# Decay rows three chunks ahead in five buffers, and six PSUM banks for the q/k/v projection, in a hybrid DeltaNet / SGU / Fourier layer

## The chip, the cores and the metric

The kernel runs on one core of a Trainium2 chip. The metric is the device time of one execution in microseconds (us). Engines are named as in the profile: PE is TensorE (matrix multiply), PEld its weight loads, DVE is VectorE, ACT is ScalarE, POOL is GpSimd, and SP is SyncE, which here only issues DMAs. Each engine works through its own instruction queue in order: an instruction that waits holds back everything behind it on its engine.

## The reference, cut to what matters

One layer processes 2048 sample tokens and 128 prompt tokens (2176 in all, D_MODEL = 1024). A combined projection feeds three token mixers (gated DeltaNet, a spatial-gating MLP, a Fourier mixer), which are gated, merged and projected out. The change lies in the preparation of the DeltaNet branch:

```python
qkv = short_conv(qkv, conv_w).astype(jnp.float32)      # qkv: 1536 columns of the projection, conv over 3 tokens, SiLU
...
g = -jnp.exp(a_log) * jax.nn.softplus(dec + dt_bias)   # log decay per token, direction and head
...
gam = jnp.cumsum(gc, axis=-1)                          # running sum inside a chunk
diff = gam[..., :, None] - gam[..., None, :]
dec_incl = jnp.where(incl, jnp.exp(jnp.where(incl, diff, 0.0)), 0.0)
```

`dec_incl` is a triangular matrix of decays for each chunk, direction (forward and backward) and head. The kernel works in chunks of 128 tokens: 17 chunks, 2 directions, 4 heads, so 17 x 8 matrices of 128 x 128.

## The kernel before, in words

**Stages.** The tokens are normalised and kept as two 16-bit halves, `xh` and `xl`; each projection is three matmuls per 128 rows of contraction (line 160, `mm`, called from `gemm_T`). After a first stage (the `z_a` gate) comes the **q/k/v stage**, lines 488 to 510: twelve column tiles `ct` of 128 channels. For each, five token blocks `TBS` (four of 512 tokens and one of 128) are multiplied into a PSUM bank of the pool `ps_mm`, which has three; ACT copies the bank to `raw` (line 500, under a higher priority), which frees it. Then come three DVE operations of the convolution (lines 503 to 505), a sigmoid on ACT in four pieces (line 508), a product on POOL in four pieces (line 509) and a DMA to DRAM (line 510). `raw` and `cy` have two buffers each. Three further PSUM pools of one bank each, `ps_chain`, `ps_lev` and `ps_out`, are handed out in turn by `bank(ps_d, ...)`; two more banks are `ps_x`.

**Decays.** The generator `decays()` (lines 403 to 485) runs beside the q/k/v stage. It computes `gam` (kept in the tile `tok`), writes it to DRAM as rows (`gamR`, line 470), and then goes through the 17 chunks. For a chunk it broadcasts the rows of `gamR` to all 128 partitions with two DMAs of 256 KB from the SP queue (line 478), runs eight 128 x 128 `scalar_tensor_tensor` on DVE (line 481: subtract `gam` of the token on the partition, then take the minimum with the triangle `neg_f` or `neg_b`), the exponential on ACT (line 483, 128 x 1024) and a DMA of 512 KB to DRAM from the ACT queue (line 484). The row buffers are two: tile `dc` for odd chunks, half of tile `XB` for even ones. Both tiles serve later steps as well (`prep`, line 537, and `base_inverse`, line 595), as do the tiles `E` and `Et` of 128 x 1024, which belong to `base_inverse` alone.

**Weights.** Each column tile needs a weight tile: `load_w` (line 180) loads 512 KB by a DMA on the SP queue into `wst` (line 183), ACT sums its squares (line 187), DVE casts the sum (line 170, `wscb`), PE adds it over the partitions with a 128 x 1 matmul (in the trace `b<-wscb,ones`), DVE forms the scale (lines 173 to 177), ACT and DVE write the two 16-bit halves (lines 189 and 190). `getw(1, 2)` at the head of a column tile asks for weights two tiles ahead.

**What sets the order.** The text of the program gives each instruction a priority by its place. `pace.tick(tn / 100)` after a block adds to an account, and each 1.2 in it advances `decays()` to its next `yield`, so that the text mixes the two. The order of each engine's queue is then fixed when the kernel is built, by a planner that keeps a clock of its own for every engine, takes what it believes ready, and prefers the earlier in the text; on the chip the queues run in that order whatever the real times are. After the stage `pace.drain()` empties `decays()`, and `delta()` (preparation of each chunk, block inverses, and the two scans) is paced in the same way beside the SGU, the Fourier and the merge stages.

Of the kernel before, what the change touches and what calls it, by code (L numbers as in the profile page):

```python
# [15 lines left out]
ALU = mybir.AluOpType  # L16
# [4 lines left out]
P = 128  # L21
# [5 lines left out]
NCH = NTOK // P  # L27
H = 4
# [5 lines left out]
XB = 4  # L34
# [11 lines left out]
_COFF = {}  # L46
# [64 lines left out]
def hybrid_flow_kernel(ctx: ExitStack, tc: tile.TileContext, x_prompt, x_sample, state_delta, c, c_ctx, ln_g, w_ada,  # L111
# [3 lines left out]
    V, A, G, PE, SY = nc.vector, nc.scalar, nc.gpsimd, nc.tensor, nc.sync  # L115
# [9 lines left out]
    def sb(pl, shape, tag, dt=F32, bufs=None):  # L125
        kw = {} if bufs is None else {"bufs": bufs}
        return pl.tile(list(shape), dt, tag=tag, name=nm(tag), **kw)
# [5 lines left out]
    ps_mm = pool(ctx, "ps_mm", 3, space=PSUM)  # L133
    ps_d = [pool(ctx, f"ps_d{i}", 1, space=PSUM) for i in range(3)]
# [4 lines left out]
    def bank(pl, shape, tag="b"):  # L139
        if pl is ps_d:  # L140
            rot[0] += 1
            pl = ps_d[rot[0] % 3]
        return pl.tile(list(shape), F32, tag=tag, name=nm(tag))
# [6 lines left out]
    cst = sb(csp, [P, _CF], "cst")  # L150
    SY.dma_start(cst, consts[:, 0:_CF])
    K = {n_: cst[:, a:b] for n_, (a, b) in _COFF.items() if b <= _CF}
# [162 lines left out]
    for blk in range(8):  # L315
# [3 lines left out]
        ps = bank(ps_d, [2, 256])  # L319
# [38 lines left out]
    for ti, (t0, tn) in enumerate(TBS):  # L358
# [13 lines left out]
        for k in range(KT):  # L372
            ps = bank(ps_d, [P, tn])
            for j in range(nt):
                PE.transpose(ps[:, j * P:(j + 1) * P], xt[:, j, k * P:(k + 1) * P], ident)
            t = sb(p0p, [P, tn], "xm", bufs=3)
# [3 lines left out]
        for g in range(4):  # L380
            ps = bank(ps_mm, [P, tn])
# [18 lines left out]
    dq = pool(dl, "dqa", 1, side="right")  # L400
    a1 = ExitStack()
    a1p = pool(a1, "a1p", 2)
    def decays():
        pbs = sb(dq, [P, NCH, 16], "sq")
        for c0, c1 in ((0, 9), (9, NCH)):
            pb = bank(ps_mm, [P, c1 - c0, 32])
            for t in range(c0, c1):
                ts = slice(t * P, (t + 1) * P)
                for k in range(KT):
                    if k == KT - 1:  # L410
                        mm(pb[:, t - c0, 0:16], xl[:, k, ts], bdp[:, k, 0:16], False, False)
                    mm(pb[:, t - c0, :], xh[:, k, ts], bdp[:, k, :], k == 0, k == KT - 1)
                    if k < KT - 1:
                        mm(pb[:, t - c0, 0:16], xl[:, k, ts], bdp[:, k, 0:16], False, False)
            A.copy(pbs[:, c0:c1, :], pb[:, :, 16:32])
            V.tensor_tensor(pbs[:, c0:c1, :], pbs[:, c0:c1, :], pb[:, :, 0:16], ALU.add)
        pbv = pbs.rearrange("p c (s d h) -> p s d c h", s=2, d=2)
        for d in range(2):
            A.activation(beta[:, d], pbv[:, 0, d], AF.Sigmoid, scale=bdw.inv)
        yield 1  # L420
        NH = 2 * NCH * H
        blob = sb(dq, [P, 2, WB], "tok").rearrange("p d x -> p (d x)")
        dec, e0, e1, e2 = [blob[:, i * 160:i * 160 + NH] for i in range(4)]
        dec = dec.rearrange("p (d c h) -> p d c h", d=2, h=H)
        for d in range(2):
            V.tensor_scalar(dec[:, d], pbv[:, 1, d], bdw.inv, None, ALU.mult)
        dtb = sb(a1p, [P, 2, H], "dtb", bufs=1)
        al = sb(a1p, [P, 2, H], "al", bufs=1)
        SY.dma_start(dtb, dt_bias.rearrange("o d h -> o (d h)").to_broadcast([P, 8]).rearrange("p (d h) -> p d h", d=2))
        SY.dma_start(al, a_log.rearrange("o d h -> o (d h)").to_broadcast([P, 8]).rearrange("p (d h) -> p d h", d=2))  # L430
        A.activation(al, al, AF.Exp)
        for d in range(2):
            V.tensor_tensor(dec[:, d], dec[:, d], dtb[:, d, :].rearrange("p (o h) -> p o h", o=1).to_broadcast([P, NCH, H]), ALU.add)
        flat = lambda t: t.rearrange("p d c h -> p (d c h)")
        V.scalar_tensor_tensor(e0, flat(dec), -1.0, flat(dec), ALU.mult, ALU.max)
        A.activation(e0, e0, AF.Exp, scale=-1.0)
        V.tensor_scalar(e1, e0, 1.0, None, ALU.add)
        A.activation(e2, e1, AF.Ln)
        V.tensor_scalar(e1, e1, -1.0, 1e-30, ALU.add, ALU.max)
        V.reciprocal(e1, e1)  # L440
        V.tensor_mul(e2, e2, e1)
        V.tensor_scalar(e1, e0, -0.5, 1.0, ALU.mult, ALU.add)
        V.tensor_tensor(e2, e2, e1, ALU.max)
        V.tensor_mul(e2, e2, e0)
        V.scalar_tensor_tensor(e2, flat(dec), 0.0, e2, ALU.max, ALU.add)
        yield 1
        gg = e1.rearrange("p (d c h) -> p d c h", d=2, h=H)
        for d in range(2):
            V.scalar_tensor_tensor(gg[:, d], e2.rearrange("p (d c h) -> p d c h", d=2, h=H)[:, d], -1.0,
                                   al[:, d, :].rearrange("p (o h) -> p o h", o=1).to_broadcast([P, NCH, H]), ALU.mult, ALU.mult)  # L450
        pg = bank(ps_d, [P, 2, NH])
        HN = NH // 2
        for d, tri in ((0, "tri_f"), (1, "tri_b")):
            mm(pg[:, 0, d * HN:(d + 1) * HN], K[tri], flat(gg)[:, d * HN:(d + 1) * HN])
        mm(pg[:, 1, :], ones, flat(gg))
        gam = e0.rearrange("p (d c h) -> p d c h", d=2, h=H)
        V.tensor_copy(flat(gam), pg[:, 0, :])
        A.activation(flat(eg), flat(gam), AF.Exp)
        A.activation(flat(egl), pg[:, 1, :], AF.Exp)
        V.tensor_tensor(flat(ed), pg[:, 1, :], flat(gam), ALU.subtract)  # L460
        A.activation(flat(ed), flat(ed), AF.Exp)
        V.tensor_scalar(flat(neg), flat(eg), -1.0, None, ALU.mult)
        yield 1
        gamR = dram("gamR", [2, NCH * H, P])
        for d in range(2):
            pt = bank(ps_d, [HN, P])
            PE.transpose(pt, flat(gam)[:, d * HN:(d + 1) * HN], ident)
            gr = sb(a1p, [HN, P], "gr", bufs=1)
            V.tensor_copy(gr, pt)
            SY.dma_start(gamR[d], gr)  # L470
        for t in range(NCH):
            if t % 2:
                row = sb(dq, [P, 2, WB], "dc")
            else:
                row = sb(dq, [P, 2048], "XB")[:, 0:1024].rearrange("p (d x) -> p d x", d=2)
            row = row.rearrange("p d (h i) -> p d h i", h=H)
            for d in range(2):
                SY.dma_start(row[:, d], gamR[d, t * H:(t + 1) * H, :].rearrange("h (o i) -> o h i", o=1).to_broadcast([P, H, P]))
            for d in range(2):
                for h in range(H):  # L480
                    V.scalar_tensor_tensor(row[:, d, h, :], row[:, d, h, :], gam[:, d, t, h:h + 1], K["neg_f" if d == 0 else "neg_b"], ALU.subtract, ALU.min)
            yield 1
            A.activation(row, row, AF.Exp)
            A.dma_start(decD[t], row.rearrange("p d h i -> p d (h i)"))
            yield 1

    pace.start(decays(), 1.2)
    for ct in range(12):
        w = getw(1, 2)
        for half in range(1):  # L490
            raw = sb(a1p, [P, LP], "raw")
            G.memset(raw[:, 0:1], 0.0)
            G.memset(raw[:, NS + 1:NS + 3], 0.0)
            G.memset(raw[:, LP - 1:LP], 0.0)
            for t0, tn in TBS:
                ps = bank(ps_mm, [P, tn])
                gemm_T(ps, w, 0, xh[:, :, t0:t0 + tn], xl[:, :, t0:t0 + tn])
                o = t0 + 1 if t0 < NS else t0 + 3
                with tc.high_priority():
                    A.activation(raw[:, o:o + tn], ps, AF.Copy, scale=w.inv)  # L500
                pace.tick(tn / 100)
            y = sb(a1p, [P, LP - 2], "cy")
            V.tensor_scalar(y, raw[:, 0:LP - 2], convw(0, ct), None, ALU.mult)
            V.scalar_tensor_tensor(y, raw[:, 1:LP - 1], convw(1, ct), y, ALU.mult, ALU.add)
            V.scalar_tensor_tensor(y, raw[:, 2:LP], convw(2, ct), y, ALU.mult, ALU.add)
            for c0 in range(0, LP - 2, CQ):
                c1 = min(c0 + CQ, LP - 2)
                A.activation(raw[:, 1 + c0:1 + c1], y[:, c0:c1], AF.Sigmoid)  # L508
                G.tensor_tensor(y[:, c0:c1], y[:, c0:c1], raw[:, 1 + c0:1 + c1], ALU.mult)  # L509
            G.dma_start(qkvD[ct], y)  # L510
# [350 lines left out]
    ps = bank(ps_x, [P, 4, P])  # L861
# [6 lines left out]
    for t in range(NCH):  # L868
        ps = bank(ps_mm, [P, 4, P])
# [10 lines left out]
        ps = bank(ps_x, [P, 4, P])  # L880
# [7 lines left out]
    for g in range(4):  # L888
        uw, zw = getw(2, 2)
        for ti, (t0, tn) in enumerate(TBS):  # L890
            st = sb(ep, [P, tn], "st", bufs=3)
            SY.dma_start(st, vsD[g][:, t0:t0 + tn])
            ps = bank(ps_mm, [P, tn])
# [17 lines left out]
    for g in range(4):  # L911
        xw, zw = getw(2, 2)
        for gh in range(1):
            yT = sb(fp, [P, NTOK], "yT", bufs=1)
            Y1 = sb(fp, [P, 64, 32], "Y1")
            for q in range(0, NCH, 4):
                qn = min(4, NCH - q)
                ps = bank(ps_mm, [P, qn, P])
                for i in range(qn):
                    t = q + i  # L920
# [4 lines left out]
                if q < 16:  # L925
                    ps = bank(ps_x, [P, 4, 64, 2])
# [3 lines left out]
                else:  # L930
                    ps = bank(ps_x, [P, 2 * P])
# [225 lines left out]
```

## Time and profile before

| | before |
|---|---|
| runs | 2378.42 us median of 3 (2374.1 to 2380.57) |
| profiled execution | 2377.82 us, of which the span from first to last instruction is 2376.0 us |
| mean granted TensorE clock | 0.981 |
| HBM read and written | 222.16 MB and 125.39 MB |
| q/k/v stage, first to last matmul | 153.57 to 444.04 us |
| chunks of `decays()`, first DVE operation to last store issued | 188.0 to 309.9 us |

A profile page gives, for the slowest core, the busy time of each engine, groups of instructions by line with their count, total and mean time, and the idle time of the engine just before them with what ended it. "x" counts instructions. A table of windows gives for each stretch its length, then busy time (and count) of PE, PEld, DVE, ACT and POOL, then the granted clock (1.00 is full speed), the share of the DMA engines in use and GB/s. A timeline lists start, duration, engine, line, operation and output<-inputs, and in square brackets the idle time before it and who ended it. A table of waits says who waited for whom: total us, times, longest.

### The profile page before, as it was taken

The page shows a single profiled execution, that of the slowest core. Times are in us where ns is not written, and L with a number is a line of the kernel's source. Part 1 is how long each engine was busy: PE and PEld are TensorE (multiplying, and loading weights), DVE is VectorE, ACT ScalarE, POOL GpSimd, SP SyncE. Part 2 cuts the span into 40 slices and gives each one's busy share as a digit, 9 for nine tenths or more (in the row PEclk, how much of TensorE's full clock was granted, in tenths as well). Part 3 has the DMA queues.
Part 4 walks back from the last instruction along what each step waited for, and adds up shares of the span by engine and source line. Part 5 has one row for each costly group of instructions (what it writes and reads, how often), then busy time and mean ns, then how long its engine had stood idle before and what let it go on. Part 6 is the DMA issues. An engine that isn't in the chain of part 4 may idle for free. (4 is left out here: it accounts for less than half of the span.)

```text
span 2376.0 us, 43430 instructions
## 1 busy us (share of the span) xinstructions
PE 2261.1 (95%) x17092; PEld 1376.6 (58%) x17092; DVE 1271.6 (54%) x3117; ACT 765.0 (32%) x1430; POOL 820.9 (35%) x1056
## 2 busy tenths in 40 slices
PE   7999899998989987899989999999999999999998
PEld 3554444798545676679656656656665444444443
DVE  5635743568575856655574556674654242332453
ACT  3444543322333332332332222242332242221331
POOL 2421122342434431345423233445552212122543
PEclk9999999999999998999999999999999999999999
DMA  8315632375857672244453445565563253332542
GB/s 278 129 50 174 226 110 76 109 254 132 241 138 237 190 181 58 82 139 131 138 181 124 129 138 158 162 201 178 160 182 109 95 163 119 113 97 80 189 151 98
DMA packets 353238, 350.40 MB, mean 147 GB/s; under 512 B 70929, under 2 KB 273674, under 8 KB 351498
## 3 DMA queue, kind: packets, MB, share of 16 engines
q1 hardware_dynamic: 338986, 294.13, 41.9%
q0 software_dynamic: 9152, 40.13, 4.3%
q10 hardware_dynamic: 4896, 13.37, 1.5%
q8 instruction: 134, 2.20, 0.4%
q14 instruction: 70, 0.57, 0.1%
HBM read 222.16 MB, written 125.39 MB: 146 GB/s over the span
## 5 line engine op out<-in xcount | busy, mean ns | idle before, releaser
L160 PE MATMUL b<-xh,whi 128*128 128x512 f16 (+1 forms) x2080 | 707.2, 350 | 18.5 <-ACT raw L500 11.6
L160 PE MATMUL b<-xl,whi 128*128 128x512 f16 (+1 forms) x2080 | 708.5, 350 | 0.1
L160 PE MATMUL b<-xh,wlo 128*128 128x512 f16 (+1 forms) x2080 | 707.8, 350 | 0.0
L160 PEld LDWEIGHTS <-whi 128*128 128x128 f16 x4160 | 389.9, 98 | 402.0 <-issue 36.3
L160 PEld LDWEIGHTS <-wlo 128*128 128x128 f16 x2080 | 204.4, 98 | 195.8 <-issue 9.8
L160 PE MATMUL b<-big,bhi 128*128 128x512 f16 (+1 forms) x960 | 252.8, 348 | 5.7 <-ACT big L987 4.2
L1019 POOL TENSOR_TENSOR mrow<-mrow,sg 128x512 f32<-128x512 f32 (+1 forms) x80 | 87.9, 1102 | 317.0 <-DVE sg L1018 237.3
L160 PE MATMUL b<-whi,xh 128*128 128x128 f16 x1088 | 191.7, 222 | 0.6 <-DVE sg L844 0.5
L160 PE MATMUL b<-whi,xl 128*128 128x128 f16 x1088 | 191.8, 222 | 0.0
L160 PE MATMUL b<-wlo,xh 128*128 128x128 f16 x1088 | 191.8, 222 | 0.0
L160 PEld LDWEIGHTS <-xh 128*128 128x128 f16 x2312 | 179.5, 99 | 6.6 <-issue 5.8
L1009 ACT ACTIVATE sg<-b,winv 128x512 f32<-128x512 f32 (+1 forms) x120 | 74.6, 621 | 305.4 <-PE b L160 296.9
L160 PE MATMUL b<-big,blo 128*128 128x512 f16 (+1 forms) x480 | 163.8, 348 | 0.0
L1018 DVE SCALAR_TENSOR_TENSOR sg<-b,binv,sg 128x512 f32<-128x512 f32 (+1 forms) x80 | 53.5, 669 | 182.6 <-PE b L160 180.6
L752 POOL TENSOR_SCALAR skn<-skn,ed 128x128 f32<-128x128 f32 x136 | 80.5, 607 | 180.4 <-DMA skn<-kv 164.6
L160 PEld LDWEIGHTS <-bhi 128*128 128x128 f16 x960 | 89.2, 98 | 84.2 <-ACT big L987 2.4
L509 POOL TENSOR_TENSOR cy<-cy,raw 128x545 f32<-128x545 f32 (+1 forms) x48 | 55.4, 1180 | 223.6 <-ACT raw L508 223.6
L160 PEld LDWEIGHTS <-xl 128*128 128x128 f16 x1224 | 115.0, 99 | 0.4
L652 POOL TENSOR_TENSOR R<-ec,cst 128x512 f16<-128x512 f16 x68 | 72.6, 1088 | 103.6 <-PE b L160 50.5
L160 PE MATMUL b<-wohi,mh 128*128 128x512 f16 x272 | 104.2, 383 | 2.2 <-ACT mh L1064 2.2
L160 PE MATMUL b<-wohi,ml 128*128 128x512 f16 x272 | 104.1, 384 | 2.0 <-DVE ml L1065 2.0
L160 PE MATMUL b<-wolo,mh 128*128 128x512 f16 x272 | 104.2, 383 | 0.0
(369 smaller groups left out, 3714.9 us busy)
## 6 DMA issues: line engine op xcount, KB each, us to landing
wst<-in_w_in_dram SPq DMA_DIRECT2D x60, 512.0 KB
qkv<-cy POOLq DMA_DIRECT2D x12, 1089.0 KB, 4.5
mrow<-br SPq DMA_DIRECT2D x24, 512.0 KB
mrow<-mrg SPq DMA_DIRECT2D x19, 512.0 KB
mrow<-mrg SPq DMA_DIRECT2D x16, 576.0 KB
mrg<-mrow POOLq DMA_DIRECT2D x16, 576.0 KB, 3.2
dc<-dec SPq DMA_DIRECT2D x17, 512.0 KB
kq<-qkv SPq DMA_DIRECT2D x34, 256.0 KB
```

The lines of the kernel that those rows point to most:

```text
L160: PE.matmul(out, l, r, start=start, stop=stop)
L509: G.tensor_tensor(y[:, c0:c1], y[:, c0:c1], raw[:, 1 + c0:1 + c1], ALU.mult)
L652: G.tensor_tensor(dst[:, l].rearrange("p h a b c -> p h (a b) c"), wide(ec[:, :, which ^ d, l, :]), bm, ALU.mult)
L752: G.tensor_scalar(kn_[:, hs(h)], kn_[:, hs(h)], ed[:, d, t, h:h + 1], None, ALU.mult)
L1009: A.activation(sg, ps, AF.Sigmoid, scale=gw.inv)
L1018: V.scalar_tensor_tensor(sg, ps, binv[:, 1:2], sg, ALU.mult, ALU.mult)
L1019: G.tensor_tensor(mr, mr, sg, ALU.add)
```

## The change

Three things are changed.

1. **Row buffers.** The chunks take five buffers in turn instead of two: `dc`, `E`, `Et`, and the two halves of `XB`, which are one tile for two chunks. The row broadcasts of the first three chunks are issued ahead of the loop, and in the loop those of chunk t + 3 come ahead of the work on chunk t. The exponential and the store of a chunk (`flush`) come one chunk later in the text, with a `yield` on both sides of them.
2. **DVE.** The eight `scalar_tensor_tensor` of a chunk become two `tensor_tensor` of 128 x 1024 in place: a subtraction with `gam` broadcast along the tokens, and a minimum with the two triangles, which lie side by side in the constants and are broadcast over the heads.
3. **PSUM.** The blocks of the q/k/v stage take their banks alternately from `ps_d` (three banks in turn) and `ps_mm` (three): six in all.

```diff
+        negs = cst[:, _COFF["neg_f"][0]:_COFF["neg_b"][1]].rearrange("p (d o i) -> p d o i", d=2, o=1).to_broadcast([P, 2, H, P])
+
+        def rows_of(t):
+            if t % 5 == 0:
                 row = sb(dq, [P, 2, WB], "dc")
+            elif t % 5 in (1, 2):
+                row = sb(dq, [P, 1024], ("E", "Et")[t % 5 - 1]).rearrange("p (d x) -> p d x", d=2)
             else:
-                row = sb(dq, [P, 2048], "XB")[:, 0:1024].rearrange("p (d x) -> p d x", d=2)
+                if t % 5 == 3:
+                    xb[0] = sb(dq, [P, 2048], "XB")
+                row = xb[0][:, (t % 5 - 3) * 1024:(t % 5 - 2) * 1024].rearrange("p (d x) -> p d x", d=2)
...
-            for d in range(2):
-                for h in range(H):
-                    V.scalar_tensor_tensor(row[:, d, h, :], row[:, d, h, :], gam[:, d, t, h:h + 1], K["neg_f" if d == 0 else "neg_b"], ALU.subtract, ALU.min)
-            yield 1
+            return row
+
+        def flush(t, row):
             A.activation(row, row, AF.Exp)
             A.dma_start(decD[t], row.rearrange("p d h i -> p d (h i)"))
+
+        xb = [None]
+        ready = [rows_of(t) for t in range(3)]
+        yield 1
+        last = None
+        for t in range(NCH):
+            if t + 3 < NCH:
+                ready.append(rows_of(t + 3))
+            row = ready[t]
+            g4 = gam[:, :, t, :].rearrange("p d (h o) -> p d h o", o=1).to_broadcast([P, 2, H, P])
+            V.tensor_tensor(row, row, g4, ALU.subtract)
+            V.tensor_tensor(row, row, negs, ALU.min)
             yield 1
+            if last is not None:
+                flush(*last)
+            last = (t, row)
+            yield 1
+        flush(*last)
+        yield 1
...
+    flip = [0]
     pace.start(decays(), 1.2)
...
-                ps = bank(ps_mm, [P, tn])
+                flip[0] ^= 1
+                ps = bank(ps_d if flip[0] else ps_mm, [P, tn])
```

More of the change, by code (lines that the diff above doesn't have):

```diff
@@ L470, in decays @@
             SY.dma_start(gamR[d], gr)
-        for t in range(NCH):
-            if t % 2:
+        negs = cst[:, _COFF["neg_f"][0]:_COFF["neg_b"][1]].rearrange("p (d o i) -> p d o i", d=2, o=1).to_broadcast([P, 2, H, P])
+        def rows_of(t):
+            if t % 5 == 0:
                 row = sb(dq, [P, 2, WB], "dc")
-            else:
-                row = sb(dq, [P, 2048], "XB")[:, 0:1024].rearrange("p (d x) -> p d x", d=2)
+            elif t % 5 in (1, 2):
+                row = sb(dq, [P, 1024], ("E", "Et")[t % 5 - 1]).rearrange("p (d x) -> p d x", d=2)
+            else:
+                if t % 5 == 3:
+                    xb[0] = sb(dq, [P, 2048], "XB")
+                row = xb[0][:, (t % 5 - 3) * 1024:(t % 5 - 2) * 1024].rearrange("p (d x) -> p d x", d=2)
             row = row.rearrange("p d (h i) -> p d h i", h=H)
```

## The prediction, made before the changed kernel was run

> **What bounds the kernel now.** I began with the page. Section 1 shows PE busy for 95% of the span; the other engines are at about half of it or less. So only two things can shorten the run: a stretch in which PE stands idle, or one in which it runs at a lower clock.
>
> ```profile
> span 2376.0 us, 43430 instructions
> ...
> PE 2261.1 (95%) x17092; PEld 1376.6 (58%) x17092; DVE 1271.6 (54%) x3117; ACT 765.0 (32%) x1430; POOL 820.9 (35%) x1056
> ...
> L160 PE MATMUL b<-xh,whi 128*128 128x512 f16 (+1 forms) x2080 | 707.2, 350 | 18.5 <-ACT raw L500 11.6
> ```
>
> The last line is a group: 18.5 us of idle PE ahead of it, of which 11.6 ended when ACT had copied a q/k/v bank (line 500). That is the stage that the change touches. Next the windows over it, in pieces of 25 us:
>
> ```profile
> 200.00:225.00 25.00, 25.00 (x137) 12.04 (x135) 18.15 (x42) 13.34 (x20) 6.48 (x9) 1.00 0.58 194
> 225.00:250.00 25.00, 18.36 (x91) 8.39 (x90) 12.34 (x33) 10.95 (x15) 4.29 (x8) 0.86 0.54 197
> 250.00:275.00 25.00, 24.85 (x135) 12.01 (x134) 21.86 (x43) 14.69 (x19) 5.46 (x8) 1.00 0.76 251
> 275.00:300.00 25.00, 21.84 (x113) 10.27 (x111) 14.66 (x33) 11.34 (x15) 5.51 (x8) 0.93 0.64 223
> 300.00:325.00 25.00, 23.39 (x128) 11.38 (x127) 16.87 (x22) 17.07 (x25) 9.75 (x12) 1.00 0.39 129
> 325.00:350.00 25.00, 25.00 (x136) 12.06 (x135) 8.01 (x10) 8.12 (x13) 6.21 (x13) 1.00 0.25 93
> ```
>
> PE (second number) is full until 225 and again from 325; between them it loses 6.64 + 0.15 + 3.16 + 1.61 = 11.56 us, while `decays()` runs. The clock (third from the right) falls to 0.86 and 0.93 in the two windows with the long gaps. The timelines of ACT, DVE and SP show one such gap from its cause on:
>
> ```profile
> 230.70 1.60 SPq L478 DMA_DIRECT2D XB<-gamR  x2
> ...
> 236.88 2.19 DVE L481 SCALAR_TENSOR_TENSOR XB<-XB,tok,cst 128x128 f32<-128x128 f32 x8 [13.37 <-DMA XB<-gamR]
> ...
> 239.10 1.06 ACT L483 ACTIVATE XB<-XB 128x1024 f32<-128x1024 f32 x1 [8.51 <-DVE XB L481]
> 240.06 0.67 ACT L500 ACTIVATE raw<-b,winv 128x512 f32<-128x512 f32 x1
> ...
> 240.79 0.59 PE L160 MATMUL b<-xh,whi 128*128 128x512 f16 x1 [4.81 <-ACT raw L500]
> ```
>
> The row broadcast is issued only when the buffer's previous store has landed (issued at 228.0), and lands 6 us later; DVE waits 13.37 us for it; the exponential waits 8.51 us for DVE; behind it in the ACT queue stands the copy of a full bank; PE fills its three banks and stops for 4.81 us. After that gap PE runs at half speed:
>
> ```profile
> 239.00:240.00 1.00, 0.00 (x0) 0.00 (x0) 0.82 (x5) 0.90 (x1) 0.00 (x0) 0.69 0.13 47
> 242.00:243.00 1.00, 1.00 (x4) 0.43 (x3) 1.00 (x4) 0.00 (x0) 0.00 (x0) 0.50 0.27 107
> 246.00:247.00 1.00, 1.00 (x6) 0.40 (x5) 0.96 (x6) 0.19 (x1) 0.00 (x0) 0.89 0.93 377
> ```
>
> The granted clock is 0.50 until 246. In the 25 us window 0.86 means (1 - 0.86) x 25 = 3.5 us of lost clock, of which some 0.7 lies in the gap itself: 2.8. The gap of 3.16 us costs 0.07 x 25 = 1.75, again 0.15 in the gap: 1.6. Together 4.4 us. **The prize is 11.6 + 4.4 = 16.0 us.** Cross-sum: in the quiet part a column tile takes 22.08 us (355.93 to 378.02 by line 173); twelve are 265 us; the stage takes 290.5; these 16 and the 272 small logit matmuls of `decays()` at 0.025 us (6.8, from 158.8 on) make up all but 2.7 of the rest.
>
> **The change, part by part.**
>
> *Rows ahead.* A buffer's turn before, from the timelines: rows issued 230.70, DVE done 239.07, exponential done and store issued 240.2, store landed and next rows issued 242.85: 12.15 us, over two buffers 6.1 us a chunk; the 17 chunks took 122 us, 7.2 each. With five buffers a turn is longer by one DVE step (the store now follows the next chunk's operations; some 4 us, an estimate from the next paragraph), 16 us over five: 3.3 us a chunk, and a little more where the two halves of `XB` come free together. The turn no longer sets the pace, DVE does. The same 34 broadcasts and 17 stores are issued, now in less time. They carry 17 x 1 MB; with weights and q/k/v stores (0.5 and 1.1 MB per 22 us) that is about 24 MB in 80 us, 300 GB/s; single microseconds of the trace show 418, so the DMA engines are busy but not the bound. On SP's queue up to six row DMAs now stand ahead of a weight load: 1.5 MB at 418 GB/s, 3.7 us later at most.
>
> *DVE.* Line 481 took 50.1 us for 17 chunks: 2.19 for eight alone, up to 5.76 beside POOL's products of line 509 (252.0 and 303.0). No row shows a 128x1024 `tensor_tensor` with broadcast inputs; the nearest is `scalar_tensor_tensor` 128x1024 (line 1128, 1.28 us; line 190, 1.28). Below, two halves of 128x512 with the start-to-start of about 0.6 give 1.2; above, one wait for a POOL product (1.14) each, 2.4. I take 1.28, and since the second needs the first's result, 0.03 between (as in the chain of lines 441 to 445): 2.6 us a chunk, 44 us in all, up to 53 if four chunks meet POOL. DVE's work is as before. Its other work per column tile is 1.36 + 2.48 + 2.48 + 1.28 + 0.75 = 8.35 of 22.08 us, 38%; so a chunk takes 2.8 / 0.62 = 4.5 us and `decays()` ends near 188 + 77 = 265 instead of 310. DVE is near full for that time; the convolutions slip, which costs nothing as long as the copies into `raw` (two buffers) fall no further behind than PSUM covers.
>
> *Six banks.* A bank is filled in 5.18 us (24 x 0.216). With three banks ACT may be late by some 10 us before PE stops, with six by some 26. The longest hold of the ACT queue was 8.51 us, from 229.90 to the copy at 240.06. With rows ahead these holds shrink, and without that the banks alone would cover them: two independent reasons for the same 11.6 us, which is why I trust this step most. New on that side: `gam`'s sums and transposes (lines 453 to 467) now share `ps_d` with the stage and may each wait for a copy: three times 0 to 0.69 us. I take 0.7.
>
> *What is late next.* On PE the matmul of line 173's weight scale stands in the queue at the end of each column tile, and needs the chain weight DMA, line 187, line 170. In the quiet part it has 10.5 us to spare (345.28 to 355.93). During `decays()` the way from one such matmul's result to the next cast was 14.3 (209.07 to 223.35), 21.7, 21.6 and 15.6 us, against 11.4 when quiet. A column tile is 22.08. So two of four turns were within half a microsecond of stopping PE, and no PSUM bank helps there. With `decays()` packed denser but shorter (three and a half tiles instead of five and a half) I take 1.3 us lost here; the bounds are 0 and, with 3 us over in each of three turns, 9. Nothing can be gained here, since these matmuls wait for nothing today.
>
> *Moved along.* POOL clears `E` at 150.9 today (line 610, 1.1 us); it must now come after the decays, on a POOL that is idle for tens of us. The preparation of chunk 0 starts when the last q/k/v store is there, so it moves with the stage.
>
> **Sum:** -16.0 + 0.7 + 1.3 = -14.0 us on the profiled execution of 2377.8: **2363.8**, say 2364. The median shown (2378.4) is 0.6 from it, so it needs no other offset.
>
> **After the stage.** From 445 on PE is busy 1843 of 1931 us; 88 us of gaps are left there, nearly all before 1000 and after single waits (8.5 us for line 934, 7.1 for `skn`, 6.3 for `qr`, 6.1 for line 844). Those queues are ordered by the planner's clock; if the stage ends earlier on that clock by another amount than on the chip, their order may shift either way. I put 0 in the sum and +-8 us in the range.
>
> **Rivals.**
> 1. *The weight chain takes the place of the bank wait.* For: the two turns of 21.6 and 21.7 us. Against: both contain waits of ACT and DVE for late rows. It gives back the 9 us above: -16 + 0.7 + 9 = -6, about 2372.
> 2. *New waits in the next stages.* Each wait of 6 to 8.5 us there also costs some 3 us of clock (as the 4.81 us gap did): 10 us each. One cancels most of the gain; with three new ones net (the point from which it is slower is between one and two) it is -14 + 30: 2394. For: the inverse and scan region (575 to 1000) has DVE above 80% in many windows and PE right behind it. Against: the order of the text there is unchanged.
> 3. *The same re-sorting takes gaps away* there: one or two of them, 2350.
> 4. *The change does not do what it says*: the planner issues the rows no earlier, since `XB` is one tile for two chunks, and ACT's queue holds the copies longer than six banks cover. It would need holds above 26 us: 2378.
> 5. *Bank turning itself costs clock.* In the quiet part three banks are turned with the clock at 1.00 and PE at 25.00 of 25.00, and nothing in the trace speaks for a loss. If each of the 60 changes of bank cost the 1.5 us of the shorter half-speed stretch, it would be 90 us: 2454. The Trainium skill, "TensorE: Matmul & The Clock Gate", section "A second HAM failure mode: psum-queue depth-cycling", reports such a kernel, whose clock swung between half and full as it cycled through banks; by that rule this change would be a loss, and the quiet windows here do not agree with it.
>
> **How the numbers follow.** Forecast 0.60 (2356 to 2371), rival 1 0.18, rival 2 0.09, rival 3 0.08, rival 4 0.04, rival 5 0.01. A measurement of this kernel can tell about 0.3%, 7.1 us, from no change: 2371.3 to 2385.5. Faster: 0.58 of the forecast, 0.08 of rival 3, 0.06 of rival 1: 0.72. Slower: most of rival 2 and rival 5, 0.08. Same: 0.20. Eight in ten: from 2353 (part of rival 3) to 2378 (rival 1 and the less lucky half of the drift).
>
> **What would show each step.** PE's waits for line 500 gone (below 1 us), and 225 to 300 at 25.00 busy and clock 1.00; last q/k/v matmul near 430 instead of 444; two DVE operations a chunk at 1.2 to 1.35 us and the last exponential near 265; the weight matmul's waits small; from the end of the stage to the end of the run 1931 +- 8 us. I am wrong if PE waits on `wscb` inside the stage for more than 5 us, if copies still stop PE, or if the part after the stage grows by more than 8 us.

## The result, and the profile after

The changed kernel takes 2358.1 us (median of 4 runs, 2355.22 to 2361.38) against 2376.26 us for the kernel before on the same chip (4 runs, 2373.82 to 2380.57). The ratio is 0.992 with a 95% interval of [0.990, 0.994]: 18 us less, where 14 were forecast. The profiled execution took 2355.22 us with a span of 2353.4 us. In the comparisons of the experiments, a few runs that took far longer than the rest are left out.

In the listings that follow, lines of the old text from 497 on stand 25 lines later: the copy of a bank is now line 525, the convolution 528 to 530, the sigmoid 533, POOL's product 534. Line 484 issues the row broadcasts, lines 500 and 501 are the two wide DVE operations, line 488 the exponential, line 489 the store.

From the page of the changed kernel, the span, the engines, and two groups:

```profile
span 2353.4 us, 43324 instructions
...
PE 2253.2 (96%) x17092; PEld 1374.5 (58%) x17092; DVE 1275.4 (54%) x3015; ACT 759.8 (32%) x1426; POOL 842.9 (36%) x1056
...
L160 PE MATMUL b<-xh,whi 128*128 128x512 f16 (+1 forms) x2080 | 704.1, 348 | 7.9 <-DVE sg L869 5.2
...
L534 POOL TENSOR_TENSOR cy<-cy,raw 128x545 f32<-128x545 f32 (+1 forms) x48 | 74.9, 1585 | 180.3 <-ACT raw L533 180.3
```

In the group of line 160 the 11.6 us behind the bank copies are gone; 5.2 us behind a much later step (line 869) now head its list. The windows of the changed kernel over the same stretch (length, then PE, PEld, DVE, ACT, POOL, clock, DMA share, GB/s):

```profile
200.00:225.00 25.00, 25.00 (x136) 12.13 (x135) 24.76 (x19) 13.68 (x17) 9.00 (x8) 1.00 0.79 257
225.00:250.00 25.00, 25.00 (x137) 12.05 (x135) 25.00 (x25) 18.02 (x22) 14.59 (x8) 1.00 0.81 279
250.00:275.00 25.00, 25.00 (x155) 12.85 (x154) 21.75 (x20) 15.69 (x22) 14.87 (x12) 1.00 0.76 271
275.00:300.00 25.00, 25.00 (x136) 12.08 (x135) 12.31 (x18) 11.92 (x20) 10.25 (x15) 1.00 0.34 121
```

PE is full and the clock at 1.00 in every one of them. DVE is now full from 200 to 250, and the DMA engines carry about 80%: the same decays in fewer microseconds. All that PE waits for from 145 to 430 us, from the table of waits of the changed kernel (total, times, longest):

```profile
PE b L160 <- DVE sg L385: 1.9, 1, 1.9
PE b L160 <- DVE tok L449: 0.5, 1, 0.5
```

Neither is a copy of the stage, and neither is the weight scale. From 153.60, where the stage begins in the kernel before, to the last matmul of the stage, before and then after:

```profile
153.60:444.04 290.44, 278.21 (x1737) 138.02 (x1735) 147.14 (x287) 130.54 (x188) 58.46 (x85) 0.98 0.39 133
```

```profile
153.60:428.04 274.44, 272.04 (x1766) 137.78 (x1764) 148.83 (x188) 126.72 (x189) 79.98 (x87) 1.00 0.41 140
```

| step | forecast | in the trace |
|---|---|---|
| PE behind bank copies | 11.6 us to 0 | 11.6 us to 0 |
| half clock in the stage | 4.4 us to 0 | about 5 us to 0 (summed over windows of 2 us, gaps included); 1.7 us in a second trace, at 156 to 160 us |
| prize, as the end of the stage | -16.0 us | -16.0 us (444.04 to 428.04) |
| chunks of decays, start to end | 188 to 265 | 192.7 to 265.2, 4.3 us a chunk |
| DVE, two operations of a chunk | 2.6 us | 2.3 us alone, 4.2 beside POOL's products |
| `gam`'s steps wait for a bank copy | +0.7 us | 0 behind a copy; behind line 449 0.5 us (0.7 before), behind line 385 1.3 us more |
| weight scale stops PE | +1.3 us | 0 |
| end of the stage to the end of the run | 1931 +- 8 us | 1931.96 us before, 1925.4 us after |

The stage gave what the forecast called the prize. The other 6.6 us of the 22.6 us between the two spans lie behind the stage. There the order of the instructions is the same in both kernels on all five engines, to the end of the run: counted back from the end of the two traces, the last 15,881 of 17,092 matmuls on PE, 2,722 of 3,117 instructions on DVE before the change, 1,192 of 1,430 on ACT, 965 of 1,056 on POOL and 904 of 1,008 DMA issues on SP agree, which reaches back into the stage on each. A second trace of the changed kernel (`changed_again`, below) has 1933 us there. So the 6.6 us belong to one execution and not to the change. Most of the difference between the two traces of the changed kernel is waiting: the gaps of PE behind the stage add up to 72.9 us in the first and 79.3 in the second (76.6 before).

### The profile page after: what moved, and what is told of

Read it like the earlier page. It is cut to its first block, busy times and chain, and to the rows that moved or that the text cites. A ratio compares the mean times of both kernels' runs of the same rounds, so it can differ in the third digit from the quotient of the medians.

```text
span 2353.4 us, 43324 instructions
## 1 busy us (share of the span) xinstructions
PE 2253.2 (96%) x17092; PEld 1374.5 (58%) x17092; DVE 1275.4 (54%) x3015; ACT 759.8 (32%) x1426; POOL 842.9 (36%) x1056
## 5 line engine op out<-in xcount | busy, mean ns | idle before, releaser
L534 POOL TENSOR_TENSOR cy<-cy,raw 128x545 f32<-128x545 f32 (+1 forms) x48 | 74.9, 1585 | 180.3 <-ACT raw L533 180.3
```

## The experiments

What the prediction left to be tested is whether rows ahead and six banks are each enough, as it said, or whether they take the 16 us only together, and what then holds ACT's queue late. Each expectation says what its theories give. In the table "last copy" is the start of the last q/k/v copy in the trace, 444.2 us before the change; "waits" is what PE waited for copies in the stage (total, times, longest); the difference is that of the mean times to the kernel before, in runs on the same chip.

The start of the last copy still holds what a trace lost ahead of the stage, which differs by some 3 us between the traces. The last column is therefore counted from a matmul that all kernels run just ahead of the stage: the last one of line 375, at 148.26 us before the change. From it to the last copy each trace has 1816 matmuls, in 296.0 us before the change. "Shorter" is how much less that way takes, not counting half clock at 156 to 172 us, ahead of the first chunk (1.7 us in six of the traces, 3.4 in `rows_banks_narrow`).

| kernel | ratio, 95% interval | difference, us | last copy, us | waits, us | shorter, us |
|---|---|---|---|---|---|
| before | | | 444.2 | 11.6 (6), 4.8 | |
| banks_only | 0.9962 [0.9945, 0.9978] | -8.3 | 441.0 | 6.7 (2), 3.4 | 5.2 |
| rows_wide_three_banks | 0.9954 [0.9939, 0.9969] | -10.8 | 438.5 | 9.4 (4), 6.8 | 5.5 |
| wide_only | 0.9989 [0.9973, 1.0005] | -2.3 | 446.3 | 12.2 (5), 4.9 | 0.3 |
| rows_banks_narrow | 0.9937 [0.9913, 0.9961] | -14.9 | 431.1 | 0 | 16.5 |
| changed_again | 0.9936 [0.9924, 0.9948] | -15.5 | 428.3 | 0 | 16.5 |
| rows_only | 0.9939 [0.9924, 0.9953] | -14.9 | 436.1 | 4.8 (2), 3.7 | 10.6 |
| rows_three_banks_half_dve | 0.9920 [0.9908, 0.9933] | -19.5 | 431.0 | 3.0 (3), 1.7 | 14.3 |
| rows_wide_four_banks | 0.9939 [0.9924, 0.9955] | -14.8 | 434.0 | 3.1 (3), 1.4 | 13.9 |
| three_buffers | 0.9981 [0.9964, 0.9997] | -4.1 | 444.0 | 10.2 (5), 3.7 | 0.9 |
| five_buffers | 0.9958 [0.9941, 0.9975] | -9.1 | 436.8 | 5.4 (2), 3.1 | 9.7 |
| mm_first | 0.9924 [0.9900, 0.9947] | -17.2 | 428.9 | 0 | 17.2 |

In the first trace of the changed kernel the stage is 15.7 us shorter by this count.

### Each part alone, and all but one

**The banks alone.** The kernel before with

```diff
+    flip = [0]
...
-                ps = bank(ps_mm, [P, tn])
+                flip[0] ^= 1
+                ps = bank(ps_d if flip[0] else ps_mm, [P, tn])
```

> The kernel before with one edit: the q/k/v blocks take banks alternately from ps_d and ps_mm (six), rows and DVE operations as before. Theory (the prediction's: rows ahead and six banks are two independent covers of the same stalls): the ACT queue is still held 8.5 us by late rows, but six banks cover some 26 us, so PE's waits for the copy (11.6 us) and the low clock after them (4.4) go all the same: 12 to 16 us faster, the stage ends at 428 to 432. Rival (the rows are what matters; banks only move the hold on): PE still waits for copies, 0 to 6 us faster.

Measured: 8.3 us faster, but the stage is only 5.2 us shorter, and PE still waits 6.7 us for copies: the banks are not enough. Three more banks are up to 15.5 us of matmuls, more than the 11.6 us of waits before; the simple subtraction does not hold. The ACT timeline of this kernel shows why (here line 502 is the copy, 483 the exponential, 187 the weight's squares; copies of 512 tokens free a bank that PE fills in 5.18 us):

```profile
248.84 1.06 ACT L483 ACTIVATE XB<-XB 128x1024 f32<-128x1024 f32 x1 [6.86 <-DVE XB L481]
249.80 0.35 ACT L502 ACTIVATE raw<-b,winv 128x128 f32<-128x128 f32 x1
...
251.35 0.67 ACT L502 ACTIVATE raw<-b,winv 128x512 f32<-128x512 f32 x1
259.98 1.06 ACT L187 ACTIVATE wlo<-wst 128x1024 f16<-128x1024 f32 x1 [7.96 <-DMA wst<-in_w_in_dram]
...
267.02 0.67 ACT L502 ACTIVATE raw<-b,winv 128x512 f32<-128x512 f32 x1
...
269.04 0.69 ACT L502 ACTIVATE raw<-b,winv 128x512 f32<-128x512 f32 x1 [0.40 <-ACT XB L483]
278.18 1.06 ACT L483 ACTIVATE dc<-dc 128x1024 f32<-128x1024 f32 x1 [8.46 <-DVE dc L481]
279.15 0.67 ACT L502 ACTIVATE raw<-b,winv 128x512 f32<-128x512 f32 x1
```

No single hold (a wait of ACT with copies behind it) is above 10 us, but they follow each other (9.43 us ahead of 228.83 stands before these), and between two of them the queue has one or two copies. They are not all due to rows: the 7.96 us are a wait for a weight load, which SP issued only at 255.34. From the copy at 230.84 to the one at 299.44, 68.6 us, ACT copies 11 more blocks where PE at full speed makes 15.5 (five in 22.08 us). The reserve runs down and is not filled again. The order of the queue adds to it. Counted in the two traces, the number of bank copies that stand in ACT's queue ahead of each of the 17 exponentials:

```
before      6  6  8  8 11 12 13 15 16 17 18 21 21 22 23 25 27
banks_only  4  5  7  8  9 11 12 13 14 16 17 18 20 21 22 23 26
```

With six banks the planner puts up to three copies behind an exponential that they preceded before. The chunks come no faster (last store issued at 311.4 instead of 309.9), so these copies come later, and part of the reserve is spent by the order itself.

**Rows and wide operations, three banks.** The changed kernel without those lines:

```diff
-                flip[0] ^= 1
-                ps = bank(ps_d if flip[0] else ps_mm, [P, tn])
+                ps = bank(ps_mm, [P, tn])
```

> The changed kernel with the q/k/v blocks back on the three banks of ps_mm. Theory: the changed kernel's ACT queue goes at most 12.5 us without a copy (209.8 to 222.3) and once 9.3; three banks cover some 10, so PE loses 2 to 4 us and the kernel is 11 to 15 us faster than before. Rival (the packed decays hold ACT as much as the late rows did, and only the banks hide it): PE waits of 8 us and more for copies with low clock after them, at most 6 us faster than before.

Measured: 10.8 us faster, the stage 5.5 us shorter, 9.4 us of waits. ACT waits no longer 8 us for a row; but its timeline (line 524 copy, 532 sigmoid) has one hold of the same size with another cause:

```profile
238.18 0.68 ACT L524 ACTIVATE raw<-b,winv 128x512 f32<-128x512 f32 x1
238.88 1.28 ACT L532 ACT_TABLE_LOAD   x1
248.36 2.30 ACT L532 ACTIVATE raw<-cy 128x545 f32<-128x545 f32 x4 [8.20 <-DVE cy L529]
250.57 0.67 ACT L524 ACTIVATE raw<-b,winv 128x512 f32<-128x512 f32 x1
```

The sigmoid waits for a convolution on DVE, which has the operations of the chunks in the same queue. DVE waits in this hold too, as its timeline (line 500 is a chunk's subtraction) and the window over the hold show:

```profile
244.70 1.23 DVE L500 TENSOR_TENSOR E<-E,tok 128x1024 f32<-128x1024 f32 x1 [2.42 <-issue]
```

```profile
238.00:248.30 10.30, 10.30 (x50) 4.69 (x48) 7.88 (x6) 2.14 (x3) 0.00 (x0) 1.00 1.00 316
```

The operation at 244.70 stands ahead of the last step of the convolution. It waits, by its semaphores, for the rows of its chunk, which SP issued at 236.70 and 237.07, while the DMA engines are busy all the time (share 1.00). So of the 8.20 us, 2.42 are a late row again, 1.1 the chunk's operation, and the rest is the convolution itself. What PE waited for, from this kernel's table of waits:

```profile
PE b L160 <- ACT raw L524: 9.4, 4, 6.8
```

The longest wait, 6.8 us, follows that hold. It ends with the copy at 258.82: after the one at 250.57, ACT copies nothing for another 8.25 us, in which it has a weight's squares and three exponentials to do. Most of the lateness has moved from the rows to DVE's queue.

**The wide operations alone.** The kernel before with

```diff
+        negs = ...
...
-            for d in range(2):
-                for h in range(H):
-                    V.scalar_tensor_tensor(...)
+            g4 = gam[:, :, t, :].rearrange("p d (h o) -> p d h o", o=1).to_broadcast([P, 2, H, P])
+            V.tensor_tensor(row, row, g4, ALU.subtract)
+            V.tensor_tensor(row, row, negs, ALU.min)
```

> The kernel before with one edit: two 128x1024 operations for eight, two row buffers and three banks as before. Theory: DVE time is equal (2.4 for 2.2 us a chunk alone), the waits for late rows stay, so within 3 us of before. Rival (the wide operations lose or win at the port shared with POOL): beside POOL's products an operation takes 2.17 instead of 1.22 us and POOL is held in turn; more than 4 us of difference either way.

Measured: no difference (the interval holds 1), and the stage and its waits much as before. DVE waited for rows; doing its work on them in another form shortens nothing.

**All but the wide operations.** The changed kernel with the eight `scalar_tensor_tensor` put back:

```diff
-            g4 = ...
-            V.tensor_tensor(row, row, g4, ALU.subtract)
-            V.tensor_tensor(row, row, negs, ALU.min)
+            for d in range(2):
+                for h in range(H):
+                    V.scalar_tensor_tensor(row[:, d, h, :], ...)
```

> The changed kernel with the eight 128x128 operations back in place of the two wide ones; five buffers and six banks stay. Theory: rows and banks do the whole of it: 15 to 20 us faster than before, within 3 us of the changed kernel. Rival (the wide operations are needed, since DVE is full while the decays run): DVE falls behind and PE stops at the weight scale's matmul or for a copy, 4 us or more slower than the changed kernel.

Measured: 14.9 us faster, no wait for a copy. The stage ends 2.8 us later than in the changed kernel; its window from 150 to 175 us, ahead of the first chunk, has a clock of 0.86, that is 3.5 us lost before a wide operation could matter. Without that loss the stage is as much shorter (16.5 us) as in the changed kernel (15.7 and 16.5). So rows and banks together carry the gain.

**The rows alone**, three banks and eight narrow operations (this change without its other two parts), and **the changed kernel again** beside it, unedited:

```diff
-                flip[0] ^= 1
-                ps = bank(ps_d if flip[0] else ps_mm, [P, tn])
+                ps = bank(ps_mm, [P, tn])
...
-            g4 = ...
-            V.tensor_tensor(row, row, g4, ALU.subtract)
-            V.tensor_tensor(row, row, negs, ALU.min)
+            for d in range(2):
+                for h in range(H):
+                    V.scalar_tensor_tensor(row[:, d, h, :], ...)
```

> The changed kernel with the eight narrow operations and the three banks of ps_mm: rows three ahead alone. Theory (new, after banks_only and rows_wide_three_banks gave 9 and 11 us: with rows ahead DVE is full, the convolutions come late and hold the ACT queue at the sigmoid, and three banks do not cover that): about as rows_wide_three_banks, 8 to 13 us faster than before, PE waits of 6 to 11 us for copies. Rival (the wide operations make it, by blocking DVE and POOL for longer at a time): 15 us faster, PE waits below 4 us.

> The changed kernel once more, beside the next three on one chip. Theory: the gain is the stage's 16 us and the part after the stage only scatters by a few us from run to run (its instruction order is the same as before on every engine): ratio 0.992 to 0.994, 14 to 19 us. Rival (the part after the stage gains too, 6.6 us in the first trace): 20 us or more.

Measured: the changed kernel as expected, the rows alone between the two theories. They leave 4.8 us of waits and shorten the stage by 10.6 us, of the 16.5 us of the changed kernel beside them. With the 5.2 us of the banks alone that is about the whole: neither part is enough, and neither makes the other idle. By the runs they are 14.9 us faster, as much as the changed kernel's 15.5. The runs and the traces disagree here, and a later pair (`five_buffers`, below) shows by how much the runs can be trusted.

### Who holds ACT once the rows come early

**Half of DVE's work on the chunks left out** (the subtraction of `gam`, so the decays are not the reference's), five buffers, three banks:

```diff
-            V.tensor_tensor(row, row, g4, ALU.subtract)
             V.tensor_tensor(row, row, negs, ALU.min)
```

> rows_wide_three_banks without the subtraction of gam, so one wide operation a chunk instead of two (the decays are then not the reference's). Theory: DVE has room again, the sigmoid's wait for the convolution (8.2 and 4.2 us) shrinks and PE's waits for copies fall from 9.4 to below 3 us with three banks: 14 to 17 us faster than before. Rival (the ACT queue is held by the weights' DMA or the row DMAs, not by DVE): PE still waits 6 to 10 us, no faster than rows_wide_three_banks.

Measured: beside `rows_wide_three_banks` the waits fall from 9.4 to 3.0 us and the stage ends at 431.0 instead of 438.5, with no bank added. The sigmoids that waited 4.23 and 8.20 us for the convolution wait 0.87 and 0 us here. The 19.5 us by the runs are more than was expected. The DMA engines have no more room than there (shares 0.91 and 0.92 from 200 to 250 us, against 0.84 and 0.86), so a DVE with room takes away most of what the banks take away: it is mainly DVE that holds ACT late. The order of ACT's queue is another in this kernel too, and no run separates the two.

**One bank more**, four in turn, with rows and wide operations:

```diff
-                flip[0] ^= 1
-                ps = bank(ps_d if flip[0] else ps_mm, [P, tn])
+                flip[0] += 1
+                ps = bank(ps_chain if flip[0] % 4 == 0 else ps_mm, [P, tn])
```

> The changed kernel with four banks for the stage: three of ps_mm and ps_chain for every fourth block. Theory (each bank is a reserve of one block, 5.2 us, spent once on the lateness of the whole ACT queue): PE's waits for copies fall from 9.4 (three banks) to some 4 us, the kernel is 13 to 16 us faster than before. Rival (only the two separate pools, used alternately, help): as with three banks, 9 us or more of waits.

Measured, as the theory had it: waits of 3.1 us instead of 9.4, 6.3 us less, for a bank that holds 5.18 us of matmuls. The stage ends 4.5 us earlier than with three; by the count of the last column the gain is 8.4 us, since with the long wait its half clock goes too. Here, unlike in `banks_only`, the bank is worth its size.

### What of the rows matters: text or buffers

**Three buffers**, and **five buffers**, each in the text order of before (no broadcast ahead of the loop, no late `flush`, narrow operations, three banks):

```diff
-            if t % 2:
+            if t % 3 == 0:
                 row = sb(dq, [P, 2, WB], "dc")
             else:
-                row = sb(dq, [P, 2048], "XB")[:, 0:1024].rearrange("p (d x) -> p d x", d=2)
+                row = sb(dq, [P, 1024], ("E", "Et")[t % 3 - 1]).rearrange("p (d x) -> p d x", d=2)
```

> The kernel before with three row buffers (dc, E, Et in turn) instead of two, nothing else: text order, eight narrow operations and three banks as before. Theory (the number of buffers sets the turn: 12.15 us over three is 4.1 us a chunk instead of 6.1): the decays end near 280 to 290 instead of 310, PE's waits for copies fall from 11.6 to 5 to 8 us, 5 to 11 us faster than before. Rival (the rows must be issued ahead in the text): no change, within 4 us.

```diff
-            if t % 2:
+            if t % 5 == 0:
                 row = sb(dq, [P, 2, WB], "dc")
+            elif t % 5 in (1, 2):
+                row = sb(dq, [P, 1024], ("E", "Et")[t % 5 - 1]).rearrange("p (d x) -> p d x", d=2)
             else:
-                row = sb(dq, [P, 2048], "XB")[:, 0:1024].rearrange("p (d x) -> p d x", d=2)
+                if t % 5 == 3:
+                    xb = sb(dq, [P, 2048], "XB")
+                row = xb[:, (t % 5 - 3) * 1024:(t % 5 - 2) * 1024].rearrange("p (d x) -> p d x", d=2)
```

> The kernel before with the five row buffers, but the text's order of before: each chunk's rows, operations, exponential and store together, nothing ahead; eight narrow operations, three banks. The planner makes the same queues of it as of rows_only, on every engine. Theory: so it is rows_only again, 11 to 18 us faster than before, PE waits of some 5 us. Rival: none that the queues would allow; a difference of more than 4 us from rows_only would be what runs scatter.

Measured: three buffers still leave 10.2 us of waits and bring 4.1 us, less than expected, although the chunks end at 285 instead of 310. Five buffers leave 5.4 us of waits and end the stage at 436.8, as `rows_only` does (436.1). In fact the two are one program: both traces show the same order of the instructions on every engine. Broadcasts three chunks ahead in the text and a late `flush` change nothing here, which fits a planner that issues a broadcast as soon as it believes a buffer free. The number of buffers is the whole of "rows ahead" in this pair.

This pair also says what a difference is worth: the same queues measured 9.1 and 14.9 us faster than before, in two sets of runs. The ends of the stage in their traces differ by 0.7 us. Differences of runs below some 6 us are therefore not read as causes here; the stage in the traces is.

**The turn of the banks begun on the other pool**, else the changed kernel:

```diff
-    flip = [0]
+    flip = [1]
```

> The changed kernel with the alternation started on ps_mm instead of ps_d. Theory: the wait of 1.9 us for line 385 at the start of the stage (0.6 with three banks) is for a bank that the stage before still holds, and goes or moves; at most 2 us of difference from the changed kernel, 14 to 20 us faster than before. Rival (the alternation's phase decides how well the banks cover): PE waits for copies come back, 5 us or more.

Measured, as the theory had it: PE's wait behind line 385 is 0.6 us as before instead of 1.9, no wait for a copy, 17.2 us faster. Against 15.5 and 18.5 us of the changed kernel that is no difference that the runs can tell.

## Why the prediction was right, and which step failed

**What bounds the kernel: right.** The stage had a prize of 16.0 us in waits and half clock, and it ended 16.0 us earlier in both traces of the changed kernel; counted from line 375 it became 15.7 and 16.5 us shorter. On that way PE's idle time fell from 12.8 to 2.4 us in the first trace, and the half clock from 5.1 us to 0, of which some 0.7 lay inside a gap: 14.8 of the 15.7 us. The rest the traces don't resolve.

**The sum: right within its range, two small terms missed.** +1.3 for the weight scale didn't come: no wait for it inside the stage. +0.7 for banks that `gam`'s steps share with the stage didn't come either: none of them waits for a copy, and the 0.5 us behind line 449 were 0.7 before. What came is 1.3 us more behind line 385, for a matmul that now runs at 156.85 instead of 152.23. `mm_first` shows that this can go. How near one run comes to the forecast is partly luck: the first profiled execution is 8.6 us below it, with 6.6 us of that behind the stage, and the second (2362.9 us) 0.9 us.

**The step that failed** is the one that the prediction called safest: that rows ahead and six banks are "two independent reasons for the same 11.6 us, which is why I trust this step most". Each alone leaves 4.8 to 9.4 us of the 11.6, and shortens the stage by 5.2 us (banks), 10.6 (rows) or 5.5 (rows with wide operations); together they take all 16. Two things were wrong in it.

"With three banks ACT may be late by some 10 us before PE stops, with six by some 26" was compared with the longest single wait of ACT, 8.51 us. But ACT's queue is in order, and its holds and its own work add up: the banks are a reserve that is spent once, and in `banks_only` it is spent. The trace before shows it already. While the chunks ran, its longest time without a copy was 13.68 us, where ACT waits for a weight load and not for a row, and PE's first wait, 1.31 us, follows it. From the ACT timeline before (line 187 is the weight's squares):

```profile
214.20 0.67 ACT L500 ACTIVATE raw<-b,winv 128x512 f32<-128x512 f32 x1
...
220.85 1.06 ACT L187 ACTIVATE wlo<-wst 128x1024 f16<-128x1024 f32 x1 [5.98 <-DMA wst<-in_w_in_dram]
...
227.88 0.67 ACT L500 ACTIVATE raw<-b,winv 128x512 f32<-128x512 f32 x1
```

And "with rows ahead these holds shrink" left out the next holder: with the chunks closer together DVE has more to do in less time, the convolutions come late ("the convolutions slip, which costs nothing as long as the copies ... fall no further behind than PSUM covers"), and the sigmoid holds ACT for 8.20 us. "The DMA engines are busy but not the bound" held on average (shares of 0.76 to 0.81 in the changed kernel), but in that hold they were at 1.00, and a row was late by 2.42 us. With three banks PSUM doesn't cover that; with six it does. That this step failed without harm is luck: the change happened to hold both parts. In the changed kernel a hold of that length is there still, but PE doesn't notice. From its ACT timeline:

```profile
209.41 0.36 ACT L525 ACTIVATE raw<-b,winv 128x128 f32<-128x128 f32 x1
...
221.30 1.06 ACT L488 ACTIVATE E<-E 128x1024 f32<-128x1024 f32 x1 [5.22 <-DVE E L501]
222.26 0.67 ACT L525 ACTIVATE raw<-b,winv 128x512 f32<-128x512 f32 x1
```

These are 12.5 us without a copy, and the window around it is full on PE at clock 1.00.

**The wide operations: right in effect.** They were counted at no gain, and alone they bring none. With rows ahead and only three banks they even cost: 9.4 us of waits, against 4.8 and 5.4 with the narrow operations (`rows_only`, `five_buffers`). Line 481 took 50.1 us of DVE; lines 500 and 501 take 48.4. The price of 1.28 us was 1.22, and the dependency between the two cost nothing, because the planner puts another chunk's operation between them.

**Rivals.** 1 (the weight chain takes the place): none of its waits is in the stage, in either trace of the changed kernel. 2 and 3 (re-sorted later stages): the order after the stage is unchanged on every engine, so neither could happen; the scatter of that part (1925 to 1934 us over the traces; 1925 and 1933 are both the changed kernel's) is not explained by any run here. 4 (the planner issues the rows no earlier): half true, in that the text order does nothing, but the buffers do. 5 (turning banks costs clock): fell, with 25.00 of 25.00 us busy at 1.00 in four windows in which six banks are turned. The page that it was drawn from, the Trainium skill, "TensorE: Matmul & The Clock Gate", section "A second HAM failure mode: psum-queue depth-cycling", describes a PE that idles briefly between groups of matmuls; here PE doesn't idle when it changes banks, and this trace shows no such loss.

**What stays open.** How the gain divides between the parts within some 6 us by the runs; how much of DVE's lateness in `rows_wide_three_banks` is its work and how much the order of ACT's queue; and why the run behind the stage scatters by 8 us with the same queues. No kernel here that computes the same is measurably faster than the changed one.

## What to carry to other kernels

Where an in-order queue is late again and again, more buffers behind it are a reserve that is spent once: add up the holds and the work that the queue does between them, and don't compare the reserve with the longest hold. When a wait goes, look at the engine that is then full, and at who queues behind it; two remedies for one stall may be needed together, because each leaves or brings out another holder. Where a planner fixes the order, count buffers before moving text: in the one pair tried here the same buffers gave the same queues whatever the text order, and more banks made it put the copies later. To compare a stage between traces, count it from an instruction that all of them share just ahead of it.

## What the runs showed of the hardware

A DVE operation of 128 x 1024 with two inputs in SBUF, one of them broadcast, takes 1.22 us, and the next starts 1.13 us after it. Beside a product on POOL the same operation takes 2.17, and POOL's products take far longer. The DVE timeline of the changed kernel:

```profile
192.67 1.23 DVE L500 TENSOR_TENSOR dc<-dc,tok 128x1024 f32<-128x1024 f32 x1 [6.65 <-DMA dc<-gamR]
193.82 1.22 DVE L500 TENSOR_TENSOR E<-E,tok 128x1024 f32<-128x1024 f32 x1
194.95 1.22 DVE L501 TENSOR_TENSOR dc<-dc,cst 128x1024 f32<-128x1024 f32 x1
...
217.01 2.17 DVE L500 TENSOR_TENSOR Et<-Et,tok 128x1024 f32<-128x1024 f32 x1
219.10 2.17 DVE L501 TENSOR_TENSOR E<-E,cst 128x1024 f32<-128x1024 f32 x1
```

and POOL's in the same stretch:

```profile
212.15 8.04 POOL L534 TENSOR_TENSOR cy<-cy,raw 128x545 f32<-128x545 f32 x4 [61.49 <-ACT raw L533]
```

Every DVE operation of that size inside these 8.04 us is a slow one, and the four products take 8.04 us where four alone take some 4.6 (48 in 55.4 us before, line 509). In the next two column tiles the four take 13.81 and 11.80 us, with single products of 7.93 and 5.53. Over the kernel, line 534 went from 55.4 to 74.9 us on POOL: a DVE that is kept busy slows POOL, and POOL slows it. The Trainium skill, "SBUF — State Buffer", section "Who interferes with whom", says that VectorE and GpSimd share one pair of SBUF ports under an exclusive lock; the rows above agree. It cost nothing in the changed kernel, where POOL has 180 us of idle time ahead of these products and PE waits for no copy. In `rows_wide_three_banks` four operations of 2.17 us, from 249.38 to 257.83, run ahead of the copy at 258.82, on which PE's 6.8 us end, and two exponentials in front of that copy wait 1.12 and 1.03 us for them.

The waits for copies also show when the clock fell. In all traces together, from 195 us to the end of the stage, each of the eleven waits of 3.09 us or more came with a granted clock of 0.50 for 3.4 or 6.8 us, which began between 2.6 us before the end of the wait and 1.3 us after it. No wait of 2.53 us or less did. So a long wait costs twice.
